# Building the routing one-hots of four tokens with one comparison, and giving the freed engine time to the weights' low halves

## The chip, the cores and the metric

The kernel runs on one core of a Trainium2 chip. The metric is the device time of one execution in microseconds (us); below, a time is the median of the runs shown.

## The reference, cut to what matters

The reference is a chain of two network blocks. The change touches one layer of the first: a product-key mixture of 16384 tiny experts (8 heads, 2 x 128 keys, 16 experts picked per head and token), for 512 tokens of width 1024.

```python
q = (hb @ wq).reshape(PEER_BLOCK, PEER_HEADS, 2, PEER_DKEY // 2)
s = jnp.einsum('thsd,snd->thsn', q, subkeys).astype(jnp.float32)
s1, i1 = lax.top_k(s[:, :, 0], PEER_TOPK)
s2, i2 = lax.top_k(s[:, :, 1], PEER_TOPK)
cand = (s1[..., :, None] + s2[..., None, :]).reshape(...)
sc, ci = lax.top_k(cand, PEER_TOPK)
e1 = jnp.take_along_axis(i1, ci // PEER_TOPK, axis=-1)
e2 = jnp.take_along_axis(i2, ci % PEER_TOPK, axis=-1)
gate = jax.nn.softmax(sc, axis=-1)
act = gelu(einsum('td,thkd->thk', hb, u_tab[e1 * 128 + e2])) * gate
return einsum('thk,thkd->td', act, v_tab[e1 * 128 + e2])
```

## The kernel before

**Dense instead of gathered.** For tokens 128 to 511 the kernel does not gather experts. It computes gelu(h u) for all 16384 experts in 128 blocks of 128 experts (`peer_act`), multiplies by a matrix W (expert by token) that holds the gates and is zero elsewhere, and multiplies by v (`peer_dense`). The first 128 tokens do gather their rows (`peer_own`, "own" below): GpSimd issues an indirect DMA for each of 256 rows, four ahead (`pfr`, L1111), and VectorE takes a dot product (L1119) or adds the scaled row (L1127).

**The stage of the change.** `peer_select` walks through the first NU = 56 blocks. One block is 24 TensorE matmuls of 384 columns on a 128x1024 tile of `pu`. Since the arithmetic is fp32 in three products, each tile is split: ScalarE rounds the high half (`wdH`, `weH`, L294) and another engine subtracts to get the low half (`wdL`, `weL`, L295; "low" below). For the first three blocks that engine is GpSimd, then VectorE: `peer_act(..., 0, NU, 3)`, whose last argument is `pool`. After each block the loop takes three steps of the generator `routing` and one row of "own".

**Routing.** For each t of 0 to 3, `topk` picks the experts of 128 tokens: VectorE finds maxima, GpSimd adds the candidates (`tkc`, L1215) and multiplies by the index tables (`tkeq`, L1247, four times per t, each between a VectorE comparison and a VectorE sum L1248). For t of 1 to 3 three transposes on TensorE (L1256) and a ScalarE copy (L1257) then put e1, e2 and the gate into `eT`, one column per token. After that come 32 steps of four tokens, here called a wave. For each token TensorE multiplies a plain one-hot of e2 (`oh2`) by a one-hot of e1 scaled by the gate (`oh1`), 128x128 each; ScalarE copies the four products into W (L1202). The views of the profile print both one-hots as `oh`. Of the four plain one-hots two are made by GpSimd, one by VectorE (L1198) and one by ScalarE, as relu(1 - abs(e2 - i)), in two passes (L1195, L1196). VectorE makes all four gated ones (L1200).

**What sets the order.** A scheduler orders the instructions of each engine when the program is built; each engine then runs its list strictly in order and waits on semaphores. A changed line can so move many instructions that it does not name. Weight tiles rotate through few buffers: two `wraw` (two tiles each), two `wd`, one `we`.

Of the kernel before, what the change touches and what calls it, by code (L numbers as in the profile page):

```python
# [9 lines left out]
F32 = mybir.dt.float32  # L10
# [5 lines left out]
OP = mybir.AluOpType  # L16
# [17 lines left out]
NU = 56  # L34
# [218 lines left out]
class Kern:  # L253
# [877 lines left out]
    def peer_select(self, f2, own):  # L1131


        nc, tc, ap = self.nc, self.tc, self.ap
        mov = [(T, lambda k: f2[0][:, k], lambda k: f2[1][:, k])]
        self.geD = self.dram.tile([NU, 128, TD], F32, name='geD')
        with self.tc.tile_pool(name='pk', bufs=1, reuse_waits='tile') as pk:
            sk = pk.tile([128, 2, 128], F32, name='sk')
            nc.sync.dma_start(sk.rearrange('p a b -> p (a b)'), ap['skT'])
            io = pk.tile([128, 128], F32, name='iota')  # L1140
            nc.gpsimd.iota(io, pattern=[[1, 128]], base=0, channel_multiplier=0, allow_small_or_imprecise_dtypes=True)
            eT = pk.tile([128, 3, TD], F32, name='eT')
            V = [pk.tile([128, 16, 16], F32, name=f'tkV{t}') for t in range(4)]
            I = [pk.tile([128, 16, 16], U32, name=f'tkI{t}') for t in range(4)]

            def evac(j, pss):
                q = pk.tile([128, T], F32, name='q', bufs=2)
                nc.scalar.copy(q, pss[0])
                ps = self.mmps('sa', 2)
                for t in range(4):  # L1150
                    nc.tensor.matmul(ps[:, t * 128:t * 128 + 128], q[:, t * 128:t * 128 + 128], sk[:, j % 2], start=True, stop=True)
                for t in range(4):
                    s = ps[:, t * 128:t * 128 + 128]
                    s2 = pk.tile([128, 128], F32, name='tks', bufs=2)
                    nc.vector.max(V[t][:, j, 0:8], s)
                    nc.vector.max_index(I[t][:, j, 0:8], V[t][:, j, 0:8], s)
                    nc.vector.match_replace(s2, V[t][:, j, 0:8], s, -3.0e38)
                    nc.vector.max(V[t][:, j, 8:16], s2)
                    nc.vector.max_index(I[t][:, j, 8:16], V[t][:, j, 8:16], s2)

            self.dense(ap['wq'], 0, 16, 8, mov, evac, head=3, l_eng=nc.gpsimd)
            steps = self.routing(pk, V, I, eT, io)
            n = self.taken = 0
            for b, ge in self.peer_act(pk, f2, 0, NU, 3):
                nc.sync.dma_start(self.geD[b], ge)
                if b < 4:
                    next(self.mods)
                for _ in range(-(-STEPS // NU)):
                    next(steps, None)
                    n += 1  # L1170
                if n > 9:
                    next(own)
                    self.taken += 1
            for _ in steps:
                pass
            if 'eT' in self.dbg:
                self.out_dbg('eT', eT)

    def routing(self, tp, V, I, eT, io):

        nc = self.nc
        for t in range(4):
            yield from self.topk(tp, V[t], I[t], eT, t, io)
            for b in range(4 * t - 4, 4 * t):
                if t == 0:
                    break
                w = tp.tile([128, 128, 32], F32, name='W', bufs=2)
                for q in range(8):
                    ps = self.mmps('sa', 2)
                    c0 = b * 32 + q * 4  # L1190
                    o2 = tp.tile([128, 4, 128], F32, name='oh2', bufs=3)
                    for i in range(4):
                        e2 = eT[:, 1, c0 + i:c0 + i + 1]
                        if i == 3:
                            nc.scalar.activation(o2[:, i], io, AF.Abs, scale=-1.0, bias=e2)  # L1195
                            nc.scalar.activation(o2[:, i], o2[:, i], AF.Relu, scale=-1.0, bias=1.0)  # L1196
                        else:
                            (nc.gpsimd, nc.vector)[i // 2].tensor_scalar(o2[:, i], io, e2, None, op0=OP.is_equal)  # L1198
                        o1 = tp.tile([128, 128], F32, name='oh1', bufs=4)
                        nc.vector.tensor_scalar(o1, io, eT[:, 0, c0 + i:c0 + i + 1], eT[:, 2, c0 + i:c0 + i + 1], op0=OP.is_equal, op1=OP.mult)  # L1200
                        nc.tensor.matmul(ps[:, i * 128:i * 128 + 128], o2[:, i], o1, start=True, stop=True)
                    nc.scalar.copy(w[:, :, q * 4:q * 4 + 4].rearrange('p e t -> p t e'), ps.rearrange('p (t e) -> p t e', t=4))  # L1202
                    yield
                nc.sync.dma_start(self.WD[:, b], w)

    def topk(self, tp, V, I, eT, t, io):
        nc = self.nc
        If = tp.tile([128, 8, 2, 16], F32, name='tkIf', bufs=2)
        nc.vector.tensor_copy(If.rearrange('p a b c -> p (a b) c'), I)
        Vv = V.rearrange('p (h s) a -> p h s a', s=2)  # L1210
        sc = tp.tile([128, 8, 16], F32, name='tksc', bufs=2)
        ci = tp.tile([128, 8, 16], U32, name='tkci', bufs=2)
        for h in range(8):
            cand = tp.tile([128, 16, 16], F32, name='tkc', bufs=2)
            nc.gpsimd.tensor_tensor(cand, Vv[:, h, 0, :, None].to_broadcast([128, 16, 16]),  # L1215
                                    Vv[:, h, 1, None, :].to_broadcast([128, 16, 16]), op=OP.add)
            c = cand.rearrange('p a b -> p (a b)')
            c2 = tp.tile([128, 256], F32, name='tkc2', bufs=2)
            nc.vector.max(sc[:, h, 0:8], c)
            nc.vector.max_index(ci[:, h, 0:8], sc[:, h, 0:8], c)  # L1220
            nc.vector.match_replace(c2, sc[:, h, 0:8], c, -3.0e38)
            nc.vector.max(sc[:, h, 8:16], c2)
            nc.vector.max_index(ci[:, h, 8:16], sc[:, h, 8:16], c2)
            if h % 2:
                yield
        res = tp.tile([128, 3, 128], F32, name='tkr', bufs=2)
        g = self.ownG.rearrange('p (h k) -> p h k', h=8) if t == 0 else res[:, 2].rearrange('p (h k) -> p h k', h=8)
        sm = tp.tile([128, 8], F32, name='tksm')
        nc.vector.tensor_sub(g, sc, sc[:, :, 0:1].to_broadcast([128, 8, 16]))
        nc.scalar.activation(g, g, AF.Exp)  # L1230
        nc.vector.tensor_reduce(sm, g, axis=mybir.AxisListType.X, op=OP.add)
        nc.vector.reciprocal(sm, sm)
        nc.vector.tensor_mul(g, g, sm[:, :, None].to_broadcast([128, 8, 16]))
        ab = tp.tile([128, 2, 128], U32, name='tkab')
        cif = ci.rearrange('p a b -> p (a b)')
        nc.vector.tensor_scalar(ab[:, 0], cif, 4, None, op0=OP.logical_shift_right)
        nc.vector.tensor_scalar(ab[:, 1], cif, 15, None, op0=OP.bitwise_and)
        abf = tp.tile([128, 2, 128], F32, name='tkabf')
        nc.vector.tensor_copy(abf, ab)
        for q in range(2):  # L1240
            for o in range(0, 128, 64):
                eq = tp.tile([128, 64, 16], F32, name='tkeq', bufs=2)
                s, h = slice(o, o + 64), slice(o // 16, o // 16 + 4)
                nc.vector.tensor_tensor(eq, abf[:, q, s, None].to_broadcast([128, 64, 16]),
                                        io[:, None, 0:16].to_broadcast([128, 64, 16]), op=OP.is_equal)
                e4 = eq.rearrange('p (h k) j -> p h k j', h=4)
                nc.gpsimd.tensor_tensor(e4, e4, If[:, h, q, None, :].to_broadcast([128, 4, 16, 16]), op=OP.mult)  # L1247
                nc.vector.tensor_reduce(res[:, q, s], eq, axis=mybir.AxisListType.X, op=OP.add)  # L1248
            yield
        if t == 0:  # L1250
            nc.vector.scalar_tensor_tensor(self.ownI, res[:, 0], 128.0, res[:, 1], op0=OP.mult, op1=OP.add)
            yield
            return
        ps = self.mmps('sb', 2)
        for q in range(3):
            nc.tensor.transpose(ps[:, q * 128:q * 128 + 128], res[:, q], self.ident)  # L1256
        nc.scalar.copy(eT[:, :, t * 128 - 128:t * 128], ps[:, 0:384].rearrange('p (q t) -> p q t', q=3))  # L1257
        yield

    def peer_act(self, tp, f2, first, n, pool=0, tag=('mm', 4)):  # L1260
# [1057 lines left out]
```

## Time and profile before

| | |
|---|---|
| median of 3 runs | 4587.57 us (4582.41 to 4593.75) |
| the profiled execution | 4576.06 us, of which the span of its instructions 4574.3 us |
| mean granted TensorE clock | 0.969 |
| TensorE matmul busy | 4337.6 us (95%) |
| VectorE busy | 2737.0 us (60%) |
| ScalarE busy | 1668.0 us (36%) |
| GpSimd busy | 1079.5 us (24%) |
| first to last gelu of the 56 blocks | 1010.5 to 1433.9 us |

The shares are averages over the whole program. The stage of the change is the tenth of the span from 1010 to 1438 us, and has to be read by itself.

### The profile page before, as it was taken

How to read it: one execution, taken by the hardware profiler on the slowest of the kernel's cores; microseconds unless marked ns; L12 is line 12 of the kernel's file. 1: busy time of each engine (PE TensorE's matmuls, PEld its weight loads, DVE VectorE, ACT ScalarE, POOL GpSimd, SP SyncE). 2: the span in 40 equal slices, each digit the busy share in tenths (PEclk: the TensorE clock that was granted, in tenths of full speed). 3: DMA queues.
4: the chain of work that ended last, by engine and by line, in shares of the span. 5: the costliest groups of instructions: out<-in, count | busy, mean ns of one | idle time of the engine just before them, and what ended most of it. 6: DMA issues, size and time to landing. Idle time of an engine off the chain costs nothing. (4 is left out here: it accounts for less than half of the span.)

```text
span 4574.3 us, 58699 instructions
## 1 busy us (share of the span) xinstructions
PE 4337.6 (95%) x22821; PEld 3672.4 (80%) x22821; DVE 2737.0 (60%) x5167; ACT 1668.0 (36%) x2540; POOL 1079.5 (24%) x880
## 2 busy tenths in 40 slices
PE   7898899997889999999999999999999999999998
PEld 5776788877788888888888886888888887778887
DVE  5776477599995777777543375633433376636333
ACT  3533222325663333333332265322332243223222
POOL 3222333248882333433200130100200110001001
PEclk9899899998999999999999999999999999999999
DMA  6233423336568888888423222222232210011222
GB/s 228 82 99 112 151 97 120 126 112 214 221 237 322 311 308 301 297 309 301 168 83 101 91 82 77 74 93 97 79 102 99 95 52 22 10 56 65 102 89 77
DMA packets 226771, 647.51 MB, mean 142 GB/s; under 512 B 15587, under 2 KB 81395, under 8 KB 220092
## 3 DMA queue, kind: packets, MB, share of 16 engines
q1 hardware_dynamic: 188124, 502.18, 31.7%
q0 software_dynamic: 38368, 141.58, 8.7%
q8 instruction: 180, 2.95, 0.3%
q14 instruction: 99, 0.81, 0.1%
HBM read 590.66 MB, written 53.04 MB: 141 GB/s over the span
## 5 line engine op out<-in xcount | busy, mean ns | idle before, releaser
L302 PE MATMUL mm<-xH,wdL 128*128 128x512 f32 (+4 forms) x2276 | 846.1, 373 | 19.1 <-DVE wdL L295 18.9
L300 PE MATMUL mm<-xH,wdH 128*128 128x512 f32 (+4 forms) x2276 | 850.5, 376 | 13.4 <-DVE cacc L543 8.2
L301 PE MATMUL mm<-xL,wdH 128*128 128x512 f32 (+4 forms) x2276 | 846.9, 373 | 2.0 <-POOL xL L2294 1.5
L294 ACT CAST wdH<-wraw 128x1024 fp32r<-128x1024 f32 (+2 forms) x382 | 395.1, 1035 | 1166.4 <-PE mm L301 740.3
L295 DVE TENSOR_TENSOR wdL<-wraw,wdH 128x1024 fp32r<-128x1024 f32 (+2 forms) x346 | 422.6, 1222 | 469.4 <-ACT wdH L294 450.6
L302 PEld LDWEIGHTS mm<-xH,wdL 128*128 128x128 f32 (+2 forms) x2276 | 432.7, 190 | 89.5 <-DVE wdL L295 23.6
L300 PEld LDWEIGHTS mm<-xH,wdH 128*128 128x128 f32 (+2 forms) x2276 | 432.2, 191 | 84.8 <-issue 12.1
L301 PEld LDWEIGHTS mm<-xL,wdH 128*128 128x128 f32 (+2 forms) x2276 | 433.5, 191 | 69.2 <-POOL xL L2294 3.3
L294 ACT CAST weH<-wraw 128x1024 fp32r<-128x1024 f32 (+2 forms) x162 | 168.2, 1038 | 501.3 <-PE mm L301 305.0
L295 DVE TENSOR_TENSOR weL<-wraw,weH 128x1024 fp32r<-128x1024 f32 (+1 forms) x155 | 189.8, 1225 | 240.4 <-ACT weH L294 214.8
L300 PE MATMUL mm<-xH,weH 128*128 128x512 f32 (+2 forms) x856 | 318.6, 372 | 5.5 <-ACT weH L294 4.0
L301 PE MATMUL mm<-xL,weH 128*128 128x512 f32 (+2 forms) x856 | 316.9, 370 | 1.2 <-POOL xL L2294 1.1
L302 PE MATMUL mm<-xH,weL 128*128 128x512 f32 (+2 forms) x856 | 315.9, 369 | 2.1 <-DVE weL L295 2.0
L2212 POOL TENSOR_TENSOR nsa<-r 128x512 f32<-128x512 f32 x4 | 7.7, 1935 | 1042.6 <-DVE r L1375 1042.6
L1111 POOL DMA_INDIRECT pfr<-in_pun_dram,pfI x128 | 181.2, 1416 | 296.3 <-DVE pfD L1119 204.9
L2294 POOL TENSOR_TENSOR xL<-r,xH 128x256 fp32r<-128x256 f32 (+1 forms) x84 | 69.0, 833 | 760.1 <-DVE r L2281 499.7
L1111 POOL DMA_INDIRECT pfr<-in_pv_dram,pfI x128 | 178.7, 1396 | 269.6 <-DVE pfo L1127 193.2
L1368 DVE TENSOR_TENSOR fg<-fg,mm 128x512 f32<-128x512 f32 x88 | 60.5, 688 | 283.6 <-PE mm L302 282.9
L301 PE MATMUL mm<-pVL,pGH 128*128 128x512 f32 x512 | 202.1, 395 | 6.0 <-DVE pVL L295 6.0
L302 PE MATMUL mm<-pVH,pGL 128*128 128x512 f32 x512 | 201.3, 393 | 0.0
L300 PE MATMUL mm<-pVH,pGH 128*128 128x512 f32 x512 | 196.4, 390 | 1.8 <-ACT pGH L294 1.8
L300 PEld LDWEIGHTS mm<-xH,weH 128*128 128x128 f32 x856 | 162.5, 190 | 31.6 <-ACT weH L294 4.6
(1247 smaller groups left out, 10007.9 us busy)
## 6 DMA issues: line engine op xcount, KB each, us to landing
wraw<-in_wi_dram SPq DMA_DIRECT2D x88, 1024.0 KB
praw<-in_pv_dram SPq DMA_DIRECT2D x64, 1024.0 KB
wraw<-in_pu_dram SPq DMA_DIRECT2D x63, 1024.0 KB
wraw<-in_wmod_dram SPq DMA_DIRECT2D x24, 1024.0 KB
wraw<-in_win_dram SPq DMA_DIRECT2D x24, 1024.0 KB
WD<-W SPq DMA_DIRECT2D x12, 2048.0 KB
pW<-WD SPq DMA_DIRECT2D x32, 768.0 KB
wraw<-in_wo_dram SPq DMA_DIRECT2D x16, 1024.0 KB
```

The lines of the kernel that those rows point to most:

```text
L294: nc.scalar.copy(h, x)
L295: self.last_split = (l_eng or nc.vector).tensor_sub(l, x, h.bitcast(F32)).ins
L300: mm(out, wh, xh, start=start, stop=False)
L301: mm(out, wh, xl, start=False, stop=False)
L302: mm(out, wl, xh, start=False, stop=stop)
L1111: nc.gpsimd.indirect_dma_start(out=row, out_offset=None, in_=ap[n], in_offset=bass.IndirectOffsetOnAxis(ap=self.ownI[:, k:k + 1], axis=0))
L1368: nc.vector.tensor_mul(g, g, pss[0])
L2212: self.eng.tensor_add(self.sa, r[:, 0], r[:, 1])
L2294: eng.tensor_sub(l[:, k, s], F[k], h[:, k, s].bitcast(F32))
```

## The change

The plain one-hots of a step come from one VectorE comparison over 128x512 elements (L1192). Of the four gated ones VectorE makes two (L1202) and ScalarE two, in two passes each (L1198, L1199) into tiles of their own (`oh1a`): relu(gate - gate * abs(e1 - i)). For that `eT` gets a fourth row with the negated gate, which a further ScalarE instruction writes (L1260). GpSimd makes no one-hots any more; it makes the low halves of all 56 blocks.

```diff
-            eT = pk.tile([128, 3, TD], F32, name='eT')
+            eT = pk.tile([128, 4, TD], F32, name='eT')
...
-            for b, ge in self.peer_act(pk, f2, 0, NU, 3):
+            for b, ge in self.peer_act(pk, f2, 0, NU, NU):
...
                     o2 = tp.tile([128, 4, 128], F32, name='oh2', bufs=3)
+                    nc.vector.tensor_tensor(o2, io[:, None, :].to_broadcast([128, 4, 128]),
+                                            eT[:, 1, c0:c0 + 4, None].to_broadcast([128, 4, 128]), op=OP.is_equal)
                     for i in range(4):
-                        e2 = eT[:, 1, c0 + i:c0 + i + 1]
-                        if i == 3:
-                            nc.scalar.activation(o2[:, i], io, AF.Abs, scale=-1.0, bias=e2)
-                            nc.scalar.activation(o2[:, i], o2[:, i], AF.Relu, scale=-1.0, bias=1.0)
+                        e1, gate, minus = (eT[:, q, c0 + i:c0 + i + 1] for q in (0, 2, 3))
+                        if i % 2:
+                            o1 = tp.tile([128, 128], F32, name='oh1a', bufs=3)
+                            nc.scalar.activation(o1, io, AF.Abs, scale=-1.0, bias=e1)
+                            nc.scalar.activation(o1, o1, AF.Relu, scale=minus, bias=gate)
                         else:
-                            (nc.gpsimd, nc.vector)[i // 2].tensor_scalar(o2[:, i], io, e2, None, op0=OP.is_equal)
-                        o1 = tp.tile([128, 128], F32, name='oh1', bufs=4)
-                        nc.vector.tensor_scalar(o1, io, eT[:, 0, c0 + i:c0 + i + 1], eT[:, 2, c0 + i:c0 + i + 1], op0=OP.is_equal, op1=OP.mult)
+                            o1 = tp.tile([128, 128], F32, name='oh1', bufs=3)
+                            nc.vector.tensor_scalar(o1, io, e1, gate, op0=OP.is_equal, op1=OP.mult)
...
-        nc.scalar.copy(eT[:, :, t * 128 - 128:t * 128], ps[:, 0:384].rearrange('p (q t) -> p q t', q=3))
+        nc.scalar.copy(eT[:, 0:3, t * 128 - 128:t * 128], ps[:, 0:384].rearrange('p (q t) -> p q t', q=3))
+        nc.scalar.activation(eT[:, 3, t * 128 - 128:t * 128], ps[:, 256:384], AF.Copy, scale=-1.0)
```

**What the scheduler makes of it.** ScalarE, in the second wave, the instructions of about one block (`pge` is the block's gelu, `weH` and `wdH` the high halves, W the copy of a step). Before:

```order
L294 CAST weH<-wraw 128x1024
L1273 ACTIVATE pge<-mm 128x384
L1202 COPY W<-sa 128x4x128
L1195 ACTIVATE oh_10283<-iota,eT 128x128
L1196 ACTIVATE oh_10283<-oh_10283 128x128
L1202 COPY W<-sa 128x4x128
L1195 ACTIVATE oh_10303<-iota,eT 128x128
L1196 ACTIVATE oh_10303<-oh_10303 128x128
L1202 COPY W<-sa 128x4x128
L1195 ACTIVATE oh_10323<-iota,eT 128x128
L1196 ACTIVATE oh_10323<-oh_10323 128x128
L294 CAST wdH<-wraw 128x1024
```

Now, at the same place (x2 is two instructions):

```order
L294 CAST weH<-wraw 128x1024
L1276 ACTIVATE pge<-mm 128x384
L1204 COPY W<-sa 128x4x128
L1198 ACTIVATE oh1a<-iota,eT 128x128 x2
L1199 ACTIVATE oh1a<-oh1a,eT 128x128 x2
L1198 ACTIVATE oh1a<-iota,eT 128x128
L1204 COPY W<-sa 128x4x128
L1199 ACTIVATE oh1a<-oh1a,eT 128x128
L1198 ACTIVATE oh1a<-iota,eT 128x128 x2
L1204 COPY W<-sa 128x4x128
L1199 ACTIVATE oh1a<-oh1a,eT 128x128 x2
L1198 ACTIVATE oh1a<-iota,eT 128x128
```

A step's copy of W is now followed by four passes instead of two, and the second pass of each pair reads `eT` too.

GpSimd, at the end of the first wave, where the top-k of the next 128 tokens ends. Before (`pfr` are the gathers of "own"):

```order
L1198 TENSOR_SCALAR oh_9740<-iota,eT 128x128 x2
L1215 TENSOR_TENSOR tkc<-tkV_7214 128x256 x2
L1111 DMA pfr<-in_pun_dram,pfI 128x1024
L1215 TENSOR_TENSOR tkc<-tkV_7214 128x256 x2
L1215 TENSOR_TENSOR tkc<-tkV_7215 128x256 x2
L1111 DMA pfr<-in_pun_dram,pfI 128x1024 x2
L1247 TENSOR_TENSOR tkeq<-tkeq,tkIf 128x1024 x4
```

Now:

```order
L295 TENSOR_TENSOR wdL<-wraw,wdH 128x1024
L1217 TENSOR_TENSOR tkc<-tkV_7215 128x256 x2
L295 TENSOR_TENSOR weL<-wraw,weH 128x1024
L1111 DMA pfr<-in_pun_dram,pfI 128x1024 x3
L295 TENSOR_TENSOR wdL<-wraw,wdH 128x1024
L1111 DMA pfr<-in_pun_dram,pfI 128x1024
L1249 TENSOR_TENSOR tkeq<-tkeq,tkIf 128x1024 x2
L295 TENSOR_TENSOR wdL<-wraw,wdH 128x1024
L1249 TENSOR_TENSOR tkeq<-tkeq,tkIf 128x1024
L295 TENSOR_TENSOR weL<-wraw,weH 128x1024
L1249 TENSOR_TENSOR tkeq<-tkeq,tkIf 128x1024
```

The four multiplies stood together; now lows stand between them. At the start of the same wave a low stands behind a run of gathers:

```order
L295 TENSOR_TENSOR wdL<-wraw,wdH 128x1024
L1111 DMA pfr<-in_pun_dram,pfI 128x1024 x6
L1217 TENSOR_TENSOR tkc<-tkV_7214 128x256 x4
L1111 DMA pfr<-in_pun_dram,pfI 128x1024
L1217 TENSOR_TENSOR tkc<-tkV_7214 128x256 x2
L295 TENSOR_TENSOR wdL<-wraw,wdH 128x1024
```

The low of block 13 comes after seven gathers and six candidate sums there. On TensorE the transposes of the three top-ks stood after 7.2, 20.2 and 33.2 blocks; they now stand after 10.1 (the first of the three already after 8.8), 18.0 and 31.0. The waves end after 16.0, 29.0 and 42.0 blocks before, and after 16.1, 29.0 and 42.0 now.

## Rows read from the trace of the kernel before

**Rows 1.** The page: busy time of each engine over the span.

```profile
PE 4337.6 (95%) x22821; PEld 3672.4 (80%) x22821; DVE 2737.0 (60%) x5167; ACT 1668.0 (36%) x2540; POOL 1079.5 (24%) x880
```

**Rows 2.** Windows by stage: length; PE, PEld, DVE, ACT, POOL busy; clock; DMA share; GB/s.

```profile
1010.00:1074.40 64.40, 39.68 (x236) 33.34 (x234) 53.07 (x139) 17.84 (x25) 38.75 (x24) 0.80 0.53 183
1074.40:1183.20 108.80, 92.37 (x571) 86.71 (x571) 102.81 (x280) 69.33 (x128) 89.42 (x89) 0.94 0.61 222
1183.20:1295.00 111.80, 92.53 (x571) 87.53 (x571) 102.58 (x280) 69.44 (x127) 88.25 (x87) 0.93 0.61 226
1295.00:1374.50 79.50, 76.50 (x488) 72.89 (x489) 77.53 (x192) 61.03 (x115) 75.05 (x80) 0.96 0.73 262
1374.50:1438.00 63.50, 60.50 (x346) 59.54 (x345) 26.86 (x28) 20.77 (x29) 12.89 (x9) 1.00 0.79 296
```

**Rows 3.** Groups by line and shape, 1010 to 1440 us: busy, mean ns, idle before.

```profile
L1198 POOL TENSOR_SCALAR oh<-iota,eT 128x128 f32<-128x128 f32 x192 | 166.7, 881 | 9.9 <-ACT eT L1257 5.2 <-PE mm L300 2.0 <-PE sa L1201 1.2
L1200 DVE TENSOR_SCALAR oh<-iota,eT 128x128 f32<-128x128 f32 x384 | 123.3, 384 | 6.6 <-PE sa L1201 5.3 <-ACT eT L1257 0.3
...
L295 DVE TENSOR_TENSOR wdL<-wraw,wdH 128x1024 fp32r<-128x1024 f32 x38 | 46.5, 1224 | 21.6 <-ACT wdH L294 15.6 <-PE mm L301 5.8
...
L294 ACT CAST wdH<-wraw 128x1024 fp32r<-128x1024 f32 x38 | 39.7, 1048 | 61.1 <-PE mm L301 38.7 <-DMA wraw<-in_pu_dram 20.3 <-issue 1.3
L1195 ACT ACTIVATE oh<-iota,eT 128x128 f32<-128x128 f32 x96 | 37.6, 395 | 0.1
L1196 ACT ACTIVATE oh<-oh 128x128 f32<-128x128 f32 x96 | 29.9, 315 | 2.3
...
L1198 DVE TENSOR_SCALAR oh<-iota,eT 128x128 f32<-128x128 f32 x96 | 27.4, 304 | 0.0
...
```

**Rows 4.** Timeline, first wave: start, us, what; TensorE's matmuls of a block and of steps.

```profile
1131.00 0.33 PE L301 MATMUL mm<-xL,wdH 128*128 128x384 f32 x1
1131.18 0.33 PE L302 MATMUL mm<-xH,wdL 128*128 128x384 f32 x1
...
1133.95 1.05 PE L1201 MATMUL sa<-oh,oh 128*128 128x128 f32 x8
```

**Rows 5.** Waits, 1077 to 1375 us: total, times, longest.

```profile
PE sb L1256 <- DVE tkr L1248: 21.4, 4, 7.3
```

**Rows 6.** Timeline of ScalarE in the first wave: start, us, what.

```profile
1138.97 0.39 ACT L1195 ACTIVATE oh<-iota,eT 128x128 f32<-128x128 f32 x1
1139.25 1.12 ACT L1202 COPY W<-sa 128x512 f32<-128x512 f32 x1
1140.12 0.35 ACT L1196 ACTIVATE oh<-oh 128x128 f32<-128x128 f32 x1
1140.35 0.41 ACT L1195 ACTIVATE oh<-iota,eT 128x128 f32<-128x128 f32 x1
```

**Rows 7.** ScalarE's groups by shape, whole span: two column operands, and none.

```profile
L2286 ACT ACTIVATE r<-r,V 128x256 f32<-128x256 f32 x96 | 56.6, 598 | 54.0 <-DVE r L2285 48.3 <-DVE nm L2252 5.1
...
L2198 ACT ACTIVATE nsq<-r 128x256 f32<-128x256 f32 x20 | 8.3, 414 | 40.7 <-DVE r L1375 28.2 <-DVE r L1068 6.9 <-DVE r L1410 4.1
```

**Rows 8.** Instructions of line L295 on GpSimd: ns min/median/max, first and last start.

```profile
L295 POOL TENSOR_TENSOR wdL<-wraw,wdH x36: 2349/2396/3376, 490.7 to 999.0; 128x1024 fp32r<-128x1024 f32 x36
```

**Rows 9.** Timeline of an earlier stage, GpSimd's low beside small VectorE instructions.

```profile
733.90 2.37 POOL L295 TENSOR_TENSOR wdL<-wraw,wdH 128x1024 fp32r<-128x1024 f32 x1 [9.99 <-ACT wdH L294]
734.04 0.17 DVE L420 TENSOR_SCALAR hyrv<-sa 128x16 f32<-128x16 f32 x1 [0.74 <-PE sa L970]
734.25 2.06 DVE L422 TENSOR_SCALAR hyrr<-hyrv 128x16 int32<-128x16 int32 x1
```

**Rows 10.** Instructions on the tile `pge`: ns min/median/max, first and last start.

```profile
L1298 DVE TENSOR_TENSOR pge<-pge,pW x72: 543/551/602, 1441.3 to 2266.1; 128x384 f32<-128x384 f32 x72
...
L1273 ACT ACTIVATE pge<-mm x56: 478/484/493, 1010.5 to 1433.9; 128x384 f32<-128x384 f32 x56
```

**Rows 11.** Timeline of GpSimd at the end of the first top-k wait.

```profile
1058.08 5.80 POOL L1247 TENSOR_TENSOR tkeq<-tkeq,tkIf 128x1024 f32<-128x1024 f32 x2 [1.74 <-DVE tkeq L1244]
```

## The prediction

> **What bounds the kernel now.** I read the page first: TensorE is busy 95% of the span, the other three engines far less [rows 1]. An edit that takes work off VectorE is then worth something only in a stage where TensorE waits for it. The windows by stage show such a place [rows 2]. From 1010 to 1438 us TensorE is busy 361 of 428 us, part of it at a lower granted clock (0.80 to 0.96 in the first four windows). I set the window borders at the three copies into `eT`, so the second to fourth windows are the three waves. VectorE is busy 102.8 of 108.8, 102.6 of 111.8 and 77.5 of 79.5 us in them.
>
> How much is there to win? In the timeline a block's matmul starts every 0.173 us, so a block takes 24 x 0.173 = 4.16 us, and eight matmul records of steps, which are one step, take 1.05 us [rows 3]. 56 blocks and 96 steps are 233 + 101 = 334 us; with some 9 us of small matmuls and transposes 343. The 56 gelus stretch over 424 us [rows 4]. So about 80 us (1.8%) of the stage is waiting or slow clock. The list of waits puts a good part in one place: the transposes of the second and third top-k wait 21.4 us for VectorE's last sums [rows 5]. Within a wave TensorE is close to its floor: the third has 8.8 blocks and 32 steps, 70 us, in 79.5.
>
> **VectorE's term.** Per step it made four gated and one plain one-hot; in all 123.3 + 27.4 = 150.7 us, 1.57 a step [rows 6]. Now it makes two gated ones (0.64) and a comparison of 512 elements from two SBUF inputs. The trace has no such one; between 551 ns for 384 elements [rows 4] and 1224 for 1024 [rows 6] it comes to 0.68. So 1.32 a step, 8 us less a wave. 53 lows of 1.22 us leave VectorE as well, 15.9 us in the second wave (13 blocks). It would fall from 102.6 to about 79 us there.
>
> **GpSimd's term.** It gives up 192 one-hots, 166.7 us [rows 6], and takes 53 lows at 2.39 [rows 7], 127 us. By busy time it gains. But the two engines exclude one another in places: while a GpSimd low ran, a VectorE instruction on 16 columns, of the kind that takes 0.17 us, took 2.06, ending with the low [rows 8]. The one-column-operand and two-input instructions of a wave can all be held like that. A low every block may therefore cost VectorE nothing (if it happens to run top-k maxima) or the whole 2.39 us: 13 lows are 0 to 31 us in the second wave. VectorE is in order and two thirds of its time there is work of the kinds that can be held, so I take 20: 99 us, plus the 9 us that it already waits in that window [rows 2], 108. The Trainium skill says the same of this pair (SBUF — State Buffer, Who interferes with whom): a VectorE instruction with two SBUF inputs, or in a two-port mode, and a GpSimd one that reads SBUF shut each other out for a whole instruction. By that rule alone, all 31 us would count and the second wave would take 119; the 2.06 us of [rows 8] agree with it.
>
> **ScalarE's term.** This is what I think decides. Per step it had one pair of passes and a copy; now two pairs and a copy. Back to back, the first pass occupies it 0.28 us (until the next starts), the second 0.23, the copy 0.87 [rows 9]. The second pass used constants; it now reads two columns of `eT`. Line L2286 has two column operands and takes 598 ns for 256 elements, L2198 has none and takes 414 [rows 10]: 0.18 more, so 0.41 for the pass. Added per step: 0.28 + 0.41 for the new pair and 0.18 for the old, 0.87; 28 us a wave. If the operands cost nothing it is 0.51, 16 us. I take 28, since L2286 is the nearest row. The Trainium skill (ScalarE: Activation LUTs, What ACT_TABLE_LOAD costs) gives 93 ns for each such operand, 0.19 for two; by it the term is the same.
>
> ScalarE is busy 69.3, 69.4 and 61.0 us in the waves [rows 2]. A block costs it a cast of 1.05 and a gelu of 0.48 less overlap [rows 6, 4], 1.4.
>
> **Stage by stage**, with the block counts from the order:
>
> First top-k (64.4 us before). The wait of the third block for a low that stood behind VectorE's sums goes, but GpSimd, busy 38.8 us, gets nine lows, 21.5 us; two of them stand before the third `tkeq` multiply and one before the fourth, on the chain to the transposes. With multiplies of 2.9 us [rows 11], gathers and lows in line I find `eT` some 10 us later than before. TensorE does 2.9 more blocks in that time, worth 12.1. Net -2 us (between -8 and +5).
>
> First wave. Steps 32, blocks 7.9 instead of 13.0. ScalarE: 69.3 + 28 - 5.1 x 1.4 = 90. At the end lows stand between the multiplies: four multiplies, two lows, a sum of 1.2 and the gates' product of 2.5 make 19 us from the last comparison to the transposes, in which ScalarE has some 7 us of work; 12 idle. 102 us. Before, with the blocks that now lie elsewhere taken off, 108.8 - 5.1 x 4.16 = 87.6. Net +14.5.
>
> Second wave, 13 blocks both times. ScalarE 97 and some 6 idle, 103; VectorE with GpSimd's hold 108. The later one ends it: 108 against 111.8, -4.
>
> Third wave, 11 blocks instead of 8.8. ScalarE 61.0 + 28 + 2.2 x 1.4 = 92, and 2 for its start: 94 against 79.5 + 9.2 = 88.7, +5.5.
>
> Last 14 blocks. A low on GpSimd is 1.2 us later, hidden by TensorE's 4.16 us per block since cast and low together (3.5) are shorter; if that cover is gone, because `wraw` comes free 1.2 us later per pair, it costs 7 x 1.2 = 8. I take 0. The fourth row of `eT` is three ScalarE instructions of 0.4 us at a wait, 1.2 in all, in the sums above.
>
> Sum: -2 + 14.5 - 4 + 5.5 = +14 us. On the profiled execution's 4576.06 us that is 4590; the median of the runs stands 11.5 above it, so 4587.6 + 14 = 4602 us, 0.3% slower. Nothing outside the stage changes: the same 53 rows of "own" are done in it, and the next stage's lows stay on VectorE.
>
> **Rivals.**
>
> *TensorE stays the bound and the waits shrink: faster.* For it: VectorE was the fullest engine and gets 24 us a wave back, and the order now has the next top-k's maxima between the steps instead of behind them. If the second pass takes 0.23 us as before and lows fall beside the maxima, the first wave costs 0 more, the second takes 87 + 9 = 96 (-16), the third 79 + 4 = 83 (-6), the first stage -2: -24, 4564 us. It decides if ScalarE's step stays under 2.0 us. Against it: the 598 ns of [rows 10].
>
> *GpSimd's queue: clearly slower.* A low stands behind seven gathers in the first wave, each of which needs VectorE to free a row. Where VectorE is held by lows and lows wait for VectorE, TensorE has no weights. Some 2 us for each of about 15 lows that stand behind gathers gives +30 on top of no change, with the term above up to +40: 4618 to 4628. It decides if TensorE's waits for L295 on GpSimd pass 20 us. Against it: gathers are few after the first wave's start.
>
> *No effect.* The waves are within a tenth of TensorE's floor, so both losses and gains may be covered: 4588 +- 8.
>
> **How the numbers follow.** The spread of the runs shown is 0.25%; about 0.3% (14 us) can be told from no change. My forecast, ScalarE and the VectorE-GpSimd pair as the new bounds, has a chance of 0.50 with a range of its own from 4592 to 4618; 0.32 of it is over the border of 4601, 0.18 under. The faster rival has 0.20 (0.18 beyond 0.3%), the queue 0.13, no effect 0.17 (0.02 beyond on the fast side). So faster 0.20, same 0.35, slower 0.45. The ends: below, the faster rival's own sum, half of whose 0.20 may lie still lower; above, the queue case's upper end, with half of its 0.13 beyond: 4564 to 4628 holds about eight in ten.
>
> **What the profile after would show.** Right: ScalarE busy over 90% of each wave with L1199 at about 0.5 us; L1192 at 0.68 us at best and up to 3 us where a low runs beside it; the first `eT` copy at about 1084 us; the second top-k's transposes still waiting about 10 us; TensorE waiting for `oh1a`. Wrong on ScalarE: L1199 at 0.32 us and TensorE over 95% in the waves. Wrong on GpSimd: lows of 2.4 us with VectorE's means unchanged. What would overturn the forecast most simply is a first wave of under 90 us.

## The result

A reading aid first: some group numbers in the prediction do not match the groups shown above it. Its [rows 3] is the group Rows 4, its 4 is Rows 10, its 6 is Rows 3, its 7 is Rows 8, its 8 is Rows 9, its 9 is Rows 6 and its 10 is Rows 7; the numbers 1, 2, 5 and 11 agree. Below, a group is named by the number that stands over it.

The changed kernel takes 4627.44 us (median of 5 runs, 4622.17 to 4639.69); before took 4587.57 (5 runs, 4577.46 to 4593.75). The ratio is 1.010, with a 95% interval of 1.008 to 1.012: 40 us slower by the medians, 46 by the ratio. The forecast was +14 us, 4602, and the top of its range 4628. The direction was right, the size too small by a factor of three.

The profiled execution took 4634.65 us. The gelus of the 56 blocks, beside [rows 10]:

```profile
L1276 ACT ACTIVATE pge<-mm x56: 467/487/538, 1021.3 to 1491.5; 128x384 f32<-128x384 f32 x56
```

They stretch over 470.2 us where it was 423.4, 46.8 more. (The stage starts 10.8 us later in this execution. Over the fourteen profiled executions of this document its start lies between 1010.4 and 1027.9 us, with no relation to the edit, so it is not counted to the change.) After the last of these gelus 3140 us were left before and 3141 are left now, so the loss lies in the stage. The windows by stage, with borders at the second copies into `eT` and, last, after the third wave, answer to [rows 2]:

```profile
1020.00:1097.40 77.40, 52.15 (x293) 46.83 (x290) 63.84 (x126) 22.65 (x33) 63.41 (x38) 0.85 0.60 207
1097.40:1205.50 108.10, 81.57 (x449) 70.77 (x448) 92.79 (x203) 86.99 (x182) 49.83 (x32) 0.89 0.52 182
1205.50:1330.80 125.30, 101.66 (x579) 93.64 (x578) 113.70 (x208) 95.29 (x194) 70.95 (x42) 0.92 0.57 204
1330.80:1433.00 102.20, 82.91 (x519) 76.59 (x518) 77.55 (x118) 87.75 (x184) 51.13 (x30) 0.93 0.71 258
1433.00:1496.00 63.00, 63.00 (x366) 63.00 (x365) 3.97 (x4) 22.34 (x31) 28.27 (x12) 1.00 0.58 206
```

The columns are those of Rows 2: length, then TensorE, its weight loads, VectorE, ScalarE and GpSimd busy, the clock, DMA. The reader is to see three things. No engine fills a wave any more: in the third TensorE, VectorE and ScalarE are busy 83, 78 and 88 of 102 us. VectorE, which was to gain 24 us in the second wave, is busy 113.7 there, more than before. And the granted clock is lower in all three waves than it was (0.94, 0.93, 0.96).

What TensorE waits for in the three waves (total, times, longest; us):

```profile
PE sa L1203 <- DVE oh L1202: 30.3, 16, 8.5
PE sa L1203 <- ACT W L1204: 17.0, 30, 1.1
PE sa L1203 <- ACT oh1a L1199: 7.2, 15, 2.3
PE mm L302 <- POOL wdL L295: 6.9, 3, 4.8
PE sb L1258 <- DVE tkr L1235: 2.0, 1, 2.0
PE mm L302 <- POOL weL L295: 1.8, 2, 1.1
...
PE sb L1258 <- DVE tkr L1250: 0.4, 1, 0.4
```

The 21.4 us for the transposes of the second and third top-k [rows 5] have shrunk to 2.4, as the first rival said. In their place TensorE waits 30.3 us for VectorE's gated one-hots, of which the change took half away. The groups of the stage by shape say why:

```profile
L1202 DVE TENSOR_SCALAR oh<-iota,eT 128x128 f32<-128x128 f32 x192 | 105.8, 574 | 20.5 <-PE sa L1203 19.4
L1199 ACT ACTIVATE oh1a<-oh1a,eT 128x128 f32<-128x128 f32 x192 | 86.8, 486 | 0.1
L1192 DVE TENSOR_TENSOR oh<-iota,eT 128x512 f32<-128x512 f32 x96 | 73.3, 763 | 6.4 <-PE sa L1203 5.8
L1198 ACT ACTIVATE oh1a<-iota,eT 128x128 f32<-128x128 f32 x192 | 69.4, 396 | 22.7 <-PE sa L1203 21.7 <-PE mm L302 0.9
L1119 DVE CUSTOM_DVE_ANT_0 pfr<-pfr,pfh 128x1024 f32<-128x1024 f32 x37 | 54.3, 1472 | 1.5 <-DMA pfr<-in_pun_dram,pfI 1.5
```

A gated one-hot takes 574 ns in the mean; the median is 336 and the longest 3126, by the view of the line:

```profile
L1202 DVE TENSOR_SCALAR oh<-iota,eT x192: 320/336/3126, 1101.2 to 1427.4; 128x128 f32<-128x128 f32 x192
```

A mean far above a median means that a few instructions take much longer than the rest. The timeline of one such place in the second wave (start, length; of each engine only some rows):

```profile
1256.30 2.61 DVE L1202 TENSOR_SCALAR oh<-iota,eT 128x128 f32<-128x128 f32 x2
1256.38 0.69 ACT L1198 ACTIVATE oh1a<-iota,eT 128x128 f32<-128x128 f32 x2
1256.44 2.39 POOL L295 TENSOR_TENSOR wdL<-wraw,wdH 128x1024 fp32r<-128x1024 f32 x1
...
1256.96 0.88 ACT L1199 ACTIVATE oh1a<-oh1a,eT 128x128 f32<-128x128 f32 x2
1257.73 0.40 ACT L1198 ACTIVATE oh1a<-iota,eT 128x128 f32<-128x128 f32 x1
...
1259.06 0.76 PE L1203 MATMUL sa<-oh,oh 128*128 128x128 f32 x2 [1.72 <-DVE oh L1202]
...
1261.57 1.03 ACT L1204 COPY W<-sa 128x512 f32<-128x512 f32 x1 [3.44 <-PE sa L1203]
```

GpSimd's low starts at 1256.44. Of the two one-hots of VectorE that lie there the second is held until 1258.8, when the low ends; TensorE stands 1.72 us for it, and ScalarE's copy then stands 3.44 us for TensorE. One hold is so paid on three engines. It is paid once more by the clock, in windows over the same place:

```profile
1250.00:1256.30 6.30, 5.62 (x36) 5.04 (x34) 6.30 (x23) 6.06 (x12) 1.68 (x3) 1.00 0.60 211
1256.30:1259.00 2.70, 0.66 (x3) 0.41 (x3) 2.70 (x4) 1.83 (x6) 2.53 (x2) 1.00 0.14 51
1259.00:1262.00 3.00, 2.94 (x11) 2.97 (x12) 2.90 (x11) 0.43 (x1) 0.00 (x0) 0.50 0.03 5
```

Full clock while TensorE is busy 5.62 of 6.30 us; in the hold it is busy 0.66 of 2.70; and in the 3.0 us after it, when it has work again, the granted clock is 0.50, the lower of its two levels (1.2 GHz).

### The profile page after: what moved, and what is told of

It is laid out like the page before. It is cut to its first block, busy times and chain, and to the rows that moved or that the text cites. A ratio compares the mean times of both kernels' runs of the same rounds, so it can differ in the third digit from the quotient of the medians.

```text
span 4632.8 us, 58153 instructions
## 1 busy us (share of the span) xinstructions
PE 4364.8 (94%) x22821; PEld 3686.6 (80%) x22821; DVE 2727.2 (59%) x4922; ACT 1744.7 (38%) x2735; POOL 1032.6 (22%) x741
## 5 line engine op out<-in xcount | busy, mean ns | idle before, releaser
L300 PE MATMUL mm<-xH,wdH 128*128 128x512 f32 (+4 forms) x2276 | 859.8, 380 | 10.5 <-DVE cacc L543 8.6
L295 DVE TENSOR_TENSOR wdL<-wraw,wdH 128x1024 fp32r<-128x1024 f32 (+2 forms) x310 | 377.9, 1219 | 457.1 <-ACT wdH L294 444.5
L294 ACT CAST weH<-wraw 128x1024 fp32r<-128x1024 f32 (+2 forms) x162 | 168.1, 1038 | 482.3 <-PE mm L301 295.6
L295 DVE TENSOR_TENSOR weL<-wraw,weH 128x1024 fp32r<-128x1024 f32 (+2 forms) x138 | 169.0, 1225 | 289.5 <-ACT weH L294 263.8
L295 POOL TENSOR_TENSOR wdL<-wraw,wdH 128x1024 fp32r<-128x1024 f32 x72 | 179.1, 2489 | 207.4 <-ACT wdH L294 207.0
```

What stands on the lines that cost most here:

```text
L294: nc.scalar.copy(h, x)
L295: self.last_split = (l_eng or nc.vector).tensor_sub(l, x, h.bitcast(F32)).ins
L300: mm(out, wh, xh, start=start, stop=False)
```

## The experiments

Three theories. **Lock:** a low on GpSimd holds VectorE's instructions; TensorE and ScalarE stand behind them. **ScalarE:** its two pairs of passes per step are the bound, as forecast. **Queue:** lows stand behind other work on GpSimd and come late to TensorE. All ratios are to the kernel before on the same chip, with a 95% interval.

### Undoing one part, or doing one alone

The lows back on VectorE from the fourth block on, all else as changed:

```diff
-            for b, ge in self.peer_act(pk, f2, 0, NU, NU):
+            for b, ge in self.peer_act(pk, f2, 0, NU, 3):
```

> The changed kernel with the low halves from the fourth block on back on VectorE; one comparison and ScalarE's gated one-hots stay. Lock theory (a GpSimd low holds VectorE for up to 2.4 us, TensorE stands behind it): of the about 40 us that the change cost nearly all come back, 4575 to 4595 us, and no VectorE gated one-hot is longer than 1.5 us in the waves. ScalarE theory (two pairs and a copy per step are the bound, as forecast): it stays at least 25 us over before, 4612 or more, with ScalarE over 90% busy in each wave. Queue theory (lows stand behind gathers): the same 4575 to 4595 as the lock, but then the VectorE holds in the changed kernel must have cost nothing.

Measured 1.0037 (1.0023 to 1.0051), 4599 us. No gated one-hot takes over 0.7 us any more, as the lock theory said, but the time lies between the spans of the theories: more than half of the loss comes back, and some 17 us stay with the rest of the change. All four gated ones on VectorE, the lows left on GpSimd (`eT` has three rows again, and the instruction that writes the fourth is gone):

```diff
-                        if i % 2:
-                            o1 = tp.tile([128, 128], F32, name='oh1a', bufs=3)
-                            nc.scalar.activation(o1, io, AF.Abs, scale=-1.0, bias=e1)
-                            nc.scalar.activation(o1, o1, AF.Relu, scale=minus, bias=gate)
-                        else:
-                            o1 = tp.tile([128, 128], F32, name='oh1', bufs=3)
+                        o1 = tp.tile([128, 128], F32, name='oh1', bufs=4)
...
```

> The changed kernel with all four gated one-hots on VectorE; one comparison and the lows of all 56 blocks on GpSimd stay. ScalarE theory: ScalarE's load falls below that of before, so 4575 to 4592 us. Lock theory: VectorE has two more instructions per step that a low can hold, so no better than the change, 4620 to 4660 us, with single VectorE one-hots of 1.8 to 3 us.

Measured 1.0098 (1.0082 to 1.0113), 4627 us: without any of ScalarE's passes the kernel is as slow as with two pairs, and the longest one-hot takes 2.6 us, both as the lock theory said. The comparison only, both edits above together:

> Only the one comparison: all gated one-hots on VectorE, lows as before. No lock by lows and no ScalarE pairs. VectorE does 0.68 + 4 x 0.32 = 1.96 us per step against 1.57 before, 12 us more a wave; GpSimd does no one-hots. If VectorE's sum bounds the waves: 4600 to 4625 us. If what slowed VectorE before was sharing with GpSimd's one-hots, or TensorE covers it: 4580 to 4595.

Measured 1.0031 (1.0020 to 1.0042), 4593 us. Set beside the run before it, this shows what the lows do to VectorE: on GpSimd they take 53 x 1.22 = 65 us of work off it, and yet it is busier in the waves, 323.0 of 329.0 us against 295.6 of 305.0 (columns as in Rows 2; the line of the comparison only stands further down):

```profile
1095.00:1424.00 329.00, 266.29 (x1641) 255.98 (x1641) 322.96 (x702) 157.99 (x179) 160.34 (x91) 0.91 0.57 202
```

And the kernel before with nothing but the lows on GpSimd:

```diff
-            for b, ge in self.peer_act(pk, f2, 0, NU, 3):
+            for b, ge in self.peer_act(pk, f2, 0, NU, NU):
```

> The kernel before with one edit: the lows of all 56 blocks on GpSimd. Lock theory: VectorE gets back 1.22 us a block and loses up to 2.4 in holds, and GpSimd gets 31 us a wave on top of 88 of 110: 4615 to 4660 us, TensorE waiting for L295 on GpSimd and for VectorE's one-hots. ScalarE theory: ScalarE's load is unchanged, so no slower than before, 4570 to 4592 us.

Measured 1.0124 (1.0108 to 1.0139), 4636 us. Here the lows cost twice as much, 57 us. GpSimd keeps its one-hots too and is busy 304 of 345 us from the first `eT` to the end of the steps. Two more complete a table, both with one gated one-hot of four on ScalarE (`if i == 3` for `if i % 2`), once with the lows on VectorE and once on GpSimd:

> The changed kernel with the lows back on VectorE and one of the four gated one-hots on ScalarE where two were. VectorE 0.68 + 3 x 0.32 = 1.64 us a step against 1.32, ScalarE one pair less, 0.68 a step. If ScalarE's passes are what is left of the loss (1.0037 with two pairs): 0.998 to 1.001. If VectorE's sum at the top-k is: no better than 1.003.

> Its control: the same with the one-hots of 128 columns from one run. Lock theory: 25 to 35 us over the kernel with one on ScalarE and the lows on VectorE (0.9995): 1.005 to 1.008. If the loss of the changed kernel needed ScalarE full as well: within 0.3% of before.

| gated one-hots on ScalarE, of four | lows on VectorE | lows on GpSimd | the lows' share |
|---|---|---|---|
| 0 | 1.0031 | 1.0098 | 0.67% |
| 1 | 0.9995 (0.9984 to 1.0007) | 1.0065 (1.0048 to 1.0082) | 0.70% |
| 2 | 1.0037 | 1.010 (the change) | 0.6% |

In every row the lows on GpSimd cost 0.6 to 0.7%, some 30 us of 4580, with an uncertainty of about 0.2%. The stage in the profiles agrees: it is 30, 34 and 31 us longer with them there. That is most of the loss, and this share of it does not hang on ScalarE's load. The ScalarE theory falls as the whole answer: from two pairs to none nothing is gained, in either column. But two pairs are too many and none too few, by 0.3 to 0.4% each, in both. So the second pair is the smaller part of the loss, some 16 to 19 us, as the run with one on ScalarE was to tell; the first pair gains as much as the second loses. The rest of the change is a trade between two engines that are both nearly full: with the lows on VectorE and two pairs TensorE waits for ScalarE, with none for VectorE's sums and lows. The waits of TensorE in the waves with two pairs, and then with none:

```profile
PE sa L1203 <- ACT W L1204: 11.2, 38, 0.5
PE sb L1258 <- DVE tkr L1250: 10.5, 4, 3.3
PE sa L1203 <- ACT oh1a L1199: 7.3, 31, 0.6
PE sa L1203 <- DVE oh L1202: 4.9, 3, 1.7
```

```profile
PE sb L1253 <- DVE tkr L1245: 16.9, 4, 7.3
PE mm L302 <- DVE wdL L295: 11.3, 8, 4.5
PE mm L302 <- DVE weL L295: 4.3, 3, 2.5
```

The version with one on ScalarE and the lows back is level with the kernel before; it beats the changed kernel by 1%, and no version here beats the kernel before.

### Where the lows cost

Lows on VectorE in blocks 9 to 41 alone, where the steps are; on GpSimd before and after:

```diff
+        if first == 0:
+            us = chain(self.weights(self.ap['pu'], 0, 9, 1024, l_eng=nc.gpsimd), self.weights(self.ap['pu'], 9, 33, 1024), self.weights(self.ap['pu'], 42, n - 42, 1024, l_eng=nc.gpsimd))
+        else:
+            us = chain(self.weights(self.ap['pu'], first, pool, 1024, l_eng=nc.gpsimd), self.weights(self.ap['pu'], first + pool, n - pool, 1024))
```

> The changed kernel with the lows on VectorE in blocks 9 to 41, where the steps are, and on GpSimd in the nine before and the fourteen after. Lock theory: without lows beside the one-hots it is where the kernel with all lows back was, 1.001 to 1.006 of before. If the first top-k or the last fourteen blocks carry the cost of the lows (queue and hand-over theory): 1.007 or more.

Measured 1.0055 (1.0034 to 1.0075), inside the lock theory's span; the interval overlaps that of all lows back, and the stage takes 439.0 us in its profile, where with all lows back it takes 438.9. So the cost lies chiefly in the waves; by the ratios up to some 0.2% may lie outside.

### A GpSimd instruction that nobody waits for

Queue and lock still make the same of the runs above. This one parts them: the comparison-only kernel with a second subtraction on GpSimd for each of the 53 blocks from the fourth on, whose result nothing reads (`spare` is a tile of 128x1024 bf16, set for this stage alone). On TensorE 22653 of 22821 instructions keep their place in the order.

```diff
         self.last_split = (l_eng or nc.vector).tensor_sub(l, x, h.bitcast(F32)).ins
+        if getattr(self, 'spare', None) is not None and l_eng is None and name in ('wd', 'we'):
+            nc.gpsimd.tensor_sub(self.spare, h.bitcast(F32), h.bitcast(F32))
...
```

> The comparison-only kernel (lows on VectorE, 1.0031 of before) with one more GpSimd instruction per block: a 128x1024 subtraction of the high half from itself into a tile that nothing reads. Nobody waits for its result and TensorE's order is the same but for a few places. Lock theory: it holds VectorE's one-hots as the low on GpSimd did, 30 to 60 us of holds in the waves, so 20 to 45 us more than comparison-only, 1.008 to 1.013 of before, single gated one-hots of 1.5 to 3 us. Queue theory (only a low that is late for TensorE costs): within 0.3% of comparison-only, 1.001 to 1.006.

Measured 1.0193 (1.0177 to 1.0210), 4668 us: 1.6%, some 74 us over comparison-only, well above the lock theory's own 20 to 45. The waves in one window each, of comparison-only and then of this kernel (columns as in Rows 2):

```profile
1080.00:1385.00 305.00, 262.42 (x1621) 243.81 (x1622) 295.61 (x746) 161.46 (x177) 97.92 (x59) 0.92 0.61 220
```

```profile
1099.50:1462.00 362.50, 273.04 (x1607) 247.63 (x1607) 349.73 (x740) 161.33 (x177) 170.53 (x92) 0.91 0.51 185
```

VectorE does the same work and is busy 54 us longer; the window is 57.5 us longer. GpSimd is busy less than half of it. Where VectorE is the bound, as here, the holds go into the time almost one for one. These 53 instructions cost more than the 53 lows; they take no work off VectorE, where the lows took 65 us. The view of the spare tile:

```profile
L297 POOL TENSOR_TENSOR spare<-wdH x36: 1888/1966/3126, 1038.0 to 1518.8; 128x1024 bf16<-128x1024 f32 x36
L297 POOL TENSOR_TENSOR spare<-weH x17: 1892/1966/3044, 1064.2 to 1513.1; 128x1024 bf16<-128x1024 f32 x17
...
  ACT wdH L294: 3.2, 2
```

The last row is all that waited for it: 3.2 us, two casts whose buffer it still read. That is not where 74 us went. Nor does GpSimd's own top-k work come later for it: VectorE's sums wait 7.8 us in the waves for GpSimd's multiplies, and 8.9 in comparison-only.

### The same order, another form of the one-hot

Which instructions are held? The gated one-hot is written as 129 columns, read as 3 x 43 out of a padded row of indices (column 129 is not used). The order of the four engines is the same, but for the one instruction that makes the row of indices.

```diff
+            io3 = pk.tile([128, 3, 44], F32, name='iota3')
+            nc.gpsimd.iota(io3, pattern=[[43, 3], [1, 44]], base=0, channel_multiplier=0, allow_small_or_imprecise_dtypes=True)
+            self.io3 = io3[:, :, 0:43]
...
-                        o1 = tp.tile([128, 128], F32, name='oh1', bufs=4)
-                        nc.vector.tensor_scalar(o1, io, e1, gate, op0=OP.is_equal, op1=OP.mult)
-                        nc.tensor.matmul(ps[:, i * 128:i * 128 + 128], o2[:, i], o1, start=True, stop=True)
+                        o1 = tp.tile([128, 129], F32, name='oh1', bufs=4)
+                        nc.vector.tensor_scalar(o1.rearrange('p (a b) -> p a b', a=3), self.io3, e1, gate, op0=OP.is_equal, op1=OP.mult)
+                        nc.tensor.matmul(ps[:, i * 128:i * 128 + 128], o2[:, i], o1[:, 0:128], start=True, stop=True)
```

> The kernel with all gated one-hots on VectorE and the lows on GpSimd (1.0098 of before, 42 us of holds on the one-hots in the waves), each gated one-hot written as 129 columns read as 3 x 43 out of a padded row of indices, where it was 128 from one run. The order on every engine is the same. The Trainium skill (VectorE: DVE Perf Modes, Mode 2x_2P, use both read ports for one tensor) has such an instruction, whose outer extents are odd and differ, go through one read port; by the same skill (SBUF — State Buffer, Who interferes with whom) it then isn't held by GpSimd. By rows alone: if the hold hangs on how VectorE reads its operand, no gated one-hot of over 1 us is left and 15 to 30 us come back, less some 0.07 us each for 384 slower ones: 1.003 to 1.008. If the hold is of another kind: 1.010 to 1.018 with one-hots of 1.5 to 3 us as before.

> The same 129-column one-hots in the comparison-only kernel, lows on VectorE (1.0031). This is the price of the wider, perhaps slower form by itself: 384 times 0.05 to 0.1 us on VectorE, 20 to 38 us in all, at the top-k ends and in the waves: 1.005 to 1.011. The lock theory wants the difference to the kernel with the lows on GpSimd to be under 12 us (it is 31 us with 128 columns); the queue theory wants it to stay near 30.

Measured 1.0107 (1.0090 to 1.0125) with the lows on GpSimd and 1.0079 (1.0062 to 1.0096) with them on VectorE. The difference is 0.28%, 13 us, where it is 0.67%, 31 us, with 128 columns: just over the 12 us that the lock theory allowed, and far from the queue's 30. Each such difference is uncertain by some 0.2%, so times alone part the two forms only just; the rows below part them clearly. The second kernel shows the price of the form (0.48%), so nothing is gained in all; the first missed: its time came out at the "hold of another kind" end of its expectation, while its one-hots did what the other end said. The one-hots with the lows on GpSimd, in 128 columns and then in 129, with the comparison beside the latter (minimum, median, maximum):

```profile
L1197 DVE TENSOR_SCALAR oh<-iota,eT x382: 327/335/2596, 1099.8 to 1422.3; 128x128 f32<-128x128 f32 x191
```

```profile
L1200 DVE TENSOR_SCALAR oh<-iota,eT x384: 390/395/408, 1106.5 to 1433.7; 128x129 f32<-128x129 f32 x192
...
L1195 DVE TENSOR_TENSOR oh<-iota,eT x96: 672/678/3226, 1105.9 to 1432.1; 128x512 f32<-128x512 f32 x96
```

Not one of the 384 is held any more; the longest takes 408 ns. But the low only meets the next instruction that can be held. The timeline:

```profile
1234.69 2.39 POOL L295 TENSOR_TENSOR wdL<-wraw,wdH 128x1024 fp32r<-128x1024 f32 x1
1234.72 0.39 DVE L1200 TENSOR_SCALAR oh<-iota,eT 128x129 f32<-128x129 f32 x1
1235.04 2.60 DVE L1195 TENSOR_TENSOR oh<-iota,eT 128x512 f32<-128x512 f32 x1
```

The one-hot runs through beside the low; the comparison behind it, with two inputs in SBUF, stands till the low ends. In the trace the one-hot reads 3 rows of 43 and writes one run of 129. The Trainium skill says that a VectorE instruction with one input whose outer extents are odd and differ between input and output cannot use both read ports for it (VectorE: DVE Perf Modes, Mode 2×_2P — use both read ports for one tensor). It also says that one with one SBUF input outside such a mode is not shut out by GpSimd, while one with two SBUF inputs is, by a GpSimd instruction that reads SBUF (SBUF — State Buffer, Who interferes with whom). The traces agree: 408 ns at most for the one, 3226 for the other.

What the lock theory would build, this form with one gated one-hot on ScalarE and the lows on GpSimd:

> What the lock theory would build: the changed kernel, lows of all 56 blocks on GpSimd, one gated one-hot of four on ScalarE and three on VectorE as 129 columns. VectorE per step 0.68 + 3 x 0.40 = 1.9 us but no lows: 16 us a wave less than its 1.22 per block. If only the comparison and the two-input instructions are still held (10 to 20 us in all): 0.996 to 1.003. If the hold stays: 1.007 to 1.012.

Measured 1.0070 (1.0054 to 1.0086), beside 1.0065 for its control, the same with 128 columns. A miss of the hoped-for 0.996 to 1.003: added up instruction by instruction over the median of each kind, 27 us of holds beside a low alone now lie on the comparison and 12 on the rows of "own", where in the control 35 lay on the gated one-hots and 9 on the rows; with those beside GpSimd's other work 63 us are held in all instead of 68, and the wider form costs what that saves. (Its `oh1a` tiles have two buffers, the control's three.)

### The other way round

The kernel before with VectorE's plain one-hot on ScalarE as well:

```diff
-                        if i == 3:
+                        if i > 1:
...
-                            (nc.gpsimd, nc.vector)[i // 2].tensor_scalar(o2[:, i], io, e2, None, op0=OP.is_equal)
+                            nc.gpsimd.tensor_scalar(o2[:, i], io, e2, None, op0=OP.is_equal)
```

> The kernel before with one edit the other way: VectorE's plain one-hot goes to ScalarE too (two pairs with constants in the second pass); GpSimd keeps two. VectorE is the fullest engine of the waves and loses 0.28 us a step, 9 us a wave; ScalarE gets 0.51, 16 us a wave, to 85 of 110. If VectorE's sum sets the end of each top-k: 10 to 25 us faster, 0.995 to 0.998. If TensorE or ScalarE holds: 0.998 to 1.003.

Measured 1.0022 (1.0010 to 1.0033), 4590 us. No gain, though VectorE is the fullest engine of the waves: a second pair on ScalarE does not pay here either.

## Why the prediction was too small

**VectorE's prices were right.** The comparison was put at 0.68 us and has a median of 0.68 (682 ns in the changed kernel). A gated one-hot was put at 0.32 and has a median of 0.336.

**The hold was the right mechanism, and too small in the sum.** The prediction took 20 us of holds in the second wave, out of 0 to 31, put VectorE at 99 us there, and charged holds in no other wave. The groups of VectorE in that window:

```profile
L1202 DVE TENSOR_SCALAR oh<-iota,eT 128x128 f32<-128x128 f32 x64 | 40.7, 667 | 1.5 <-PE sa L1203 1.4
L1192 DVE TENSOR_TENSOR oh<-iota,eT 128x512 f32<-128x512 f32 x32 | 24.6, 769 | 0.5 <-PE sa L1203 0.4
L1119 DVE CUSTOM_DVE_ANT_0 pfr<-pfr,pfh 128x1024 f32<-128x1024 f32 x13 | 18.5, 1427 | 1.5 <-DMA pfr<-in_pun_dram,pfI 1.5
L1246 DVE TENSOR_TENSOR tkeq<-tkabf,iota 128x1024 f32<-128x1024 f32 x4 | 7.1, 1764 | 0.0
L1123 DVE TENSOR_TENSOR pfD<-pfD,pfG 128x16 f32<-128x16 f32 x1 | 2.3, 2344 | 0.0
```

Over their undisturbed durations (0.336, 0.68, 1.22, 1.20 and 0.17) these are 19.2 + 2.8 + 2.6 + 2.3 + 2.2 = 29 us of holds. Added up instruction by instruction over those that ran beside a low alone, they are 25 us in this wave, of the 33 that its 14 lows could hold, 20 in the third and 8 to 10 in the first; the rest lay beside GpSimd's other work too. So the 20 of this wave was 9 short, and the 0 of the other two was wrong. The third wave shows it on the same line:

```profile
L1202 DVE TENSOR_SCALAR oh<-iota,eT 128x128 f32<-128x128 f32 x64 | 37.4, 609 | 9.6 <-PE sa L1203 8.9
```

VectorE's other work in the second wave is 85 us where 79 were put: five rows of "own" more fall into it. By the rule of the Trainium skill (SBUF — State Buffer, Who interferes with whom) alone, with every low counted in full, the prediction had 119 us for this wave. It took 125.3, with somewhat fewer holds than the 31 us of that rule, more other work and more idle time.

**Two steps failed: the size of the holds, and "The later one ends it".** Each wave was given one engine's sum and some idle time, 102, 108 and 94 us. They took 108.1, 125.3 and 102.2. Of the 33 us by which the stage was missed (46.8 against 14), 6 + 17 + 8 = 31 are in these three waves.

In the second wave VectorE did end it, as forecast, busy 113.7 of 125.3 us. There the miss is its own term: 99 us put, 113.7 measured, 9 of the difference holds and 6 the other work; its idle time was 11.6 us for the 9 put.

In the first and third wave no engine's sum ended it. ScalarE's was right (87 and 88 us against 90 and 92), but it idled 21 and 14 us where 12 and 2 were put, and TensorE, VectorE and ScalarE were each busy 75 to 86%. What stands in that place are the holds that were put at nothing: in the timeline above one of them is idle time on TensorE, then on ScalarE, and then a stretch at the lower clock, since a step passes VectorE, TensorE and ScalarE in turn. ScalarE's idle time is over what was put by 9 and 12 us, beside holds of some 10 and 20: they were in large part added to the larger sum and not covered by it. That few buffers between the engines make it so is likely, but no run changes their number, and it stays open.

**ScalarE's price was right, its part was not.** The first pass occupies it 0.29 us (1256.38 to 1256.96 for two, in the timeline), the second, with two columns of `eT`, 0.385 (1256.96 to 1257.73); the prediction had 0.28 and 0.41. But its sign, ScalarE over 90% busy in each wave, failed: 80, 76 and 86%. By the table the second pair costs 0.3 to 0.4%, 16 to 19 us, near the 14 that were forecast for everything, and the lows come on top with some 30. "This is what I think decides" holds for the smaller part of the loss alone. That the forecast named the right direction and a time in its range (4628 at the upper end) was part luck.

**First top-k and the last blocks.** `eT` was to come 10 us later: it came 75.6 us after the first gelu instead of 63.4, 12.2 later, and within 0.3 us of that in every kernel with the lows of all 56 blocks on GpSimd. The last 14 blocks were put at nothing: TensorE is busy 63.00 of 63.00 us there. Both were right, as far as the profiles tell. The wait for lows that was to go from the first top-k did not: it was 9.9 us and is 11.4.

**The rivals.** The queue rival had the right time, 4618 to 4628, for the wrong reason. Its sign was that TensorE's waits for GpSimd's lows pass 20 us. Over the whole stage they come to 20.1, just at that border:

```profile
PE mm L302 <- POOL wdL L295: 14.4, 5, 6.1
PE mm L302 <- POOL weL L295: 5.7, 4, 3.0
```

But before, TensorE waited 16.2 + 2.0 = 18.2 us in the stage for the lows on VectorE, so 2 us are new; 11.4 of the 20.1 lie in the first top-k; and GpSimd instructions whose result nobody needs cost 74 us. No effect was out: the interval of the ratio starts at 1.008. The faster rival's waits did shrink (21.4 to 2.4 us at the transposes), and the holds took more than that back.

## What to carry to other kernels

Busy shares say that GpSimd has room; they do not say that VectorE can run meanwhile. Before moving work to GpSimd, look at what VectorE does beside it, and charge most of each GpSimd instruction as lost to VectorE where VectorE is full of instructions with two SBUF inputs or of a kind that was seen held; here that was 25 of at most 33 us in the fullest wave. Set that against what leaves VectorE: here 65 us of lows left it, and the kernel still lost some 30. Where engines pass one step from hand to hand, expect a stall on one to be added in large part to the others' sums; here it was not hidden under the largest of them.

## What the runs showed of the hardware

53 GpSimd subtractions whose result nobody reads slowed the program by 1.6%; of 57.5 us more in the waves, VectorE was busy 54 longer with the same work. A VectorE one-hot over 129 columns in rows of 43 takes 395 ns instead of 335, and with the lows on GpSimd none of 384 was held (longest 408 ns, where 128 columns gave 2596); the hold then falls on the next instruction with two inputs (longest comparison 3226 ns). And one hold that left TensorE busy 0.66 of 2.70 us was followed by 3.0 us at a granted clock of 0.50.
